# H2 rows copied to PSUM by VectorE, outside picks marked through eight bit masks, and the first mixers' norm spread behind the next projection tile

## The chip, the cores and the metric

The kernel runs on one core of one Trainium2 chip. The metric is the time of one execution on the device in microseconds (us). A core has five engines that run side by side, each through its own list of instructions in order: TensorE (PE) multiplies matrices into PSUM, VectorE (DVE) and ScalarE (ACT) work elementwise, GpSimd (POOL) works elementwise in SBUF and issues the indirect DMAs (gathers by an index), and SyncE (SP) issues most other DMAs. They wait for each other by semaphores. An instruction that waits holds up everything behind it on its own engine.

## The reference

One layer of a decoder trunk for 512 prompt tokens and 64 sample tokens (width 2048), all in float32. What the change touches:

```python
proj = h @ w_in                               # x_lru | y_gate | sc_b | sc_c | sc_x, 1024 columns each
out_lru = rec * gelu(y_gate)                  # head group A
out_sc = sc_b * causal_conv(sc_c * sc_x)      # head group B
mix = concat([rmsnorm(out_lru, g_lru), rmsnorm(out_sc, g_sc)]) @ w_out
x = x + gate1 * mix
h2 = modulate(rmsnorm(x), shift2, scale2)
# PEER, 8 heads: 2 x 128 keys give 16384 experts of one neuron each, the best 16 a token and head
v1, i1 = top_k(scores[..., 0], 16);  v2, i2 = top_k(scores[..., 1], 16)
expert = i1 * 128 + i2                        # of the best 16 sums v1 + v2, weighted by g = softmax
out = sum(gelu(h2 . expert_u[expert]) * g * expert_v[expert])
x = x + gate2 * out                           # then a last RMSNorm
```

## The kernel before

All activations are kept with channels on the 128 partitions and tokens along the free axis. A float32 matmul is made of three passes over halves of the numbers: hi x hi, hi x lo and lo x hi, with hi made by an ACT copy and lo by a POOL subtraction (for projection weights whi and wlo, for expert weights xhi at L905 and xlo at L906).

**Projections and mixers (to about 945 us).** `project` makes one tile of 128 output channels: 96 pairs of matmuls (two halves of the tokens), 13 us of PE. For head group B each of eight steps makes the tiles c, s and b of one channel tile. Between tiles `ada_turn(n)` puts in up to n pieces of the conditioning matmuls, taken from a list of 64, of which the last seven are kept back in this part. In this stage the order on PE is written by hand; a scheduler places the other engines' instructions.

The RMSNorm of head group A is taken at the first of these steps: `norm_stats` sums the squares on PE and starts a short chain of DVE and ACT instructions on a 128x5 tile (rc_g); the function `spread` that it returns spreads the 576 reciprocal roots over all partitions by small matmuls (st_g, L237 and L239) and two ACT copies (R_g). Then DVE scales the eight tiles of o by it. The norm of group B is taken in the same way after the last step, inside the output projection.

**PEER, the U stage (1204 to 2249 us).** The 80 most used values of i1 (`perm[:L]`, L = 80) are computed densely: for each one block of 128 experts is multiplied with all 512 prompt tokens, in two halves of 24 matmuls into pu, after the second of which ACT writes act (L1377). Picks whose i1 lies outside those 80 are computed row by row: an indirect DMA from POOL (L1204) fetches for each of 128 partitions one expert's row (128x2048, one row slot of five), and DVE multiplies it with the token's H2 row and sums (the dot, L1232, one instruction a row). Rows are ordered in six tiles, of 64 rows for the samples and 34, 47, 37, 30 and 11 for the prompt. For each of the last five tiles the H2 rows of its tokens are fetched once by an indirect DMA (h2r, from a row slot) and copied to a PSUM tile hT by ACT (`use_h`, L1219). hT has one buffer, so that the copy waits for the last dot of the tile before it.

All order in this stage is written by hand in a loop over the 160 halves. It carries a reckoning of DVE time (`spare`): each half adds 5.5 or 6.9 us, rows and pieces of other work subtract what their generator yields as cost. That other work is, in turn:

- `choice`: the last top-k work, then `count`, then a sort of the tokens by how many outside picks they have;
- from its end on (half R1 of the plan), `all_slots`: the lists of rows of each tile; and the pairs of the gate matrix: one-hot tiles op and wr on DVE (L1560), scaled on ACT (L1568), multiplied on PE (gbank, L1574) and copied out by ACT (stg, L1581). They are spread evenly over the halves from R1 to half 140;
- rows, 1 a half before R1 (a little more where DVE is idle), 2 a half after it, and from the end of `all_slots` on (half R2 of the plan) evenly to the end of the stage.

`count` marks the outside picks: fl is 1 where i1 equals one of the 48 keys in `perm[:, L:]`. It reads i1 from PSUM and adds up 48 comparisons of 128x512 numbers:

```python
V.tensor_scalar(fl, i1, perm[:, L:L + 1], None, op0=ALU.is_equal)
for x in range(L + 1, 128):
    V.scalar_tensor_tensor(fl, i1, perm[:, x:x + 1], fl, op0=ALU.is_equal, op1=ALU.add)
```

**PEER, the V stage (to 3202 us).** The same blocks and the rest of the rows with the second weights, then the last norm.

Of the kernel before, what the change touches and what calls it, by code (L numbers as in the profile page):

```python
# [5 lines left out]
F32 = mybir.dt.float32  # L6
F32R = mybir.dt.float32r
I32 = mybir.dt.int32
U32 = mybir.dt.uint32
AF = mybir.ActivationFunctionType  # L10
ALU = mybir.AluOpType
# [17 lines left out]
NA = NP  # L29
NG = T - NA  # L30
NE = 128
L = 80
# [49 lines left out]
def build(ctx, tc, A, O, dbg=None):  # L82
    nc = tc.nc
    V, S, PE, G = nc.vector, nc.scalar, nc.tensor, nc.gpsimd
# [177 lines left out]

    def modulate(src, R, jscale, jshift, k0, nk, nm):

# [28 lines left out]
    x = big.tile([128, KD, T], F32, name="x", tag="big")  # L293
    for q in range(4):
        nc.sync.dma_start(x[:, 4 * q:4 * q + 4, :], A["xt"][:, 4 * q:4 * q + 4, :])
    st = []
# [55 lines left out]
    def ada_turn(n, keep=7):  # L352

        for a in pend:
            ada_out(*a)
        pend.clear()
        for _ in range(min(n, len(todo) - keep)):
            a = todo.pop(0)
            ada_mm(*a)
            if a[2] == 3:  # L360
                pend.append(a[:2])
                break
# [6 lines left out]
    for hc in range(4):  # L369
        for j in range(2):  # L370
            for kq in range(4):
                ada_mm(j, hc, kq)
                if hc == j == 0 and kq == 2:
                    spread = norm_stats(st, D, "n1")
                if hc == 0 and j == 1 and kq == 1:
                    R = spread()
# [53 lines left out]
    def project(src, nm):  # L430
        his, los = stream_w(src, nm)
        p = pp.tile([128, 2, 512], F32, name=f"pp_{nm}", tag="pp")
        mm3([p[:, 0, :HT], p[:, 1, :HT]], his, los, movs)
        return p
# [109 lines left out]
    def sc_b(i, p):  # L544
        cv = sc_t[i]
        j = KW + i
        V.tensor_mul(o[:, j, :HT], p[:, 0, :HT], cv[:, :HT])
        V.tensor_mul(o[:, j, HT:NP], p[:, 1, :NX], cv[:, HT:NP])
        V.tensor_mul(s3(o[:, j, NP:]), s3(p[:, 1, NX:HT]), smp(cv, CO, 2, 0, 8))
# [22 lines left out]
    st = []  # L572
    for i in range(KW):
        square_sum(o[:, i, :], i, st, "g0")
    for i in range(KW):
        sc_c(i, project(A["w_in"][24 + i], f"c{i}") if i else pc0)
        ada_turn(2)
        sc_x(i, project(A["w_in"][32 + i], f"s{i}"))
        if i == 0:
            spread = norm_stats(st, W, "g0")  # L580
        ada_turn(2)
        if i == 0:
            R = spread()
            st = []
            for k in range(KW):
                V.scalar_tensor_tensor(o[:, k, :], o[:, k, :], cols[:, C_GN + k:C_GN + k + 1], R, op0=ALU.mult, op1=ALU.mult)
        sc_b(i, project(A["w_in"][16 + i], f"b{i}"))
        ada_turn(2)
        square_sum(o[:, KW + i, :], i, st, "g1")
    for k in range(KW):  # L590
# [2 lines left out]
    def out_half(k, hf):  # L593
        hi, lo = half_w(A["w_out"][k], f"o{k}", hf)
        mm3([p_out[k][:, i, :HT] for i in range(2)], (hi, hi), (lo, lo), movs, range(8 * hf, 8 * hf + 8))
# [2 lines left out]
    out_half(0, 0)  # L598
    spread = norm_stats(st, W, "g1")
    out_half(1, 0)  # L600
    ada_turn(2)
    R = spread()
    for k in range(KW, KD):
        V.scalar_tensor_tensor(o[:, k, :], o[:, k, :], cols[:, C_GN + k:C_GN + k + 1], R, op0=ALU.mult, op1=ALU.mult)
        split(hv[0][:, k, :], hv[1][:, k, :], o[:, k, :], G if k % 3 == 1 else V)
# [7 lines left out]
    st = []  # L613
# [20 lines left out]
    spread = norm_stats(st, D, "n2")  # L634
    ada_turn(1, 0)
    R = spread()
# [6 lines left out]
    def pbank(tag, nm, bufs):  # L643
        return psum["p"].tile([128, 512], F32, name=nm, tag=tag, bufs=bufs)
# [39 lines left out]
    rt = p2.enter_context(tc.tile_pool(name="rt", bufs=1))  # L684
# [4 lines left out]
    perm = rt.tile([128, 128], F32, name="perm")  # L689
# [32 lines left out]
    rq = p2q.enter_context(tc.tile_pool(name="rq", bufs=1))  # L722
# [116 lines left out]
    for i in range(RB):  # L839
        r, k = new_row(f"row0_{i}")  # L840
# [146 lines left out]
    h = HD - 1  # L987
# [67 lines left out]
    def count():  # L1055

        m = nd["m"] = rt.tile([128, 3, QT], F32, name="nd_m")
        fc = rq.tile([128, 2, NA], F32, name="flags", tag="oh", bufs=2)
        fl, code = fc[:, 0, :], fc[:, 1, :]
        i1, i2 = pbank("g", "i1", 2), iselP[:, 1, :]  # L1060
        S.activation(i1, iselP[:, 0, :], AF.Copy)
        yield None
        V.tensor_scalar(fl, i1, perm[:, L:L + 1], None, op0=ALU.is_equal)
        for x in range(L + 1, 128):
            V.scalar_tensor_tensor(fl, i1, perm[:, x:x + 1], fl, op0=ALU.is_equal, op1=ALU.add)
            if x % 8 == 7:
                yield 5.0
        V.scalar_tensor_tensor(code, i1, 128.0, i2, op0=ALU.mult, op1=ALU.add)
        V.scalar_tensor_tensor(code, code, 1.0, fl, op0=ALU.add, op1=ALU.mult)
        V.tensor_reduce(m[:, 0, :], fl.rearrange("p (z k) -> p z k", k=NPK), axis=AX.X, op=ALU.add)  # L1070
        for z in range(QT):
            V.tensor_scalar(m[:, 1, z:z + 1], rowi, float(128 * z), None, op0=ALU.add)
        V.scalar_tensor_tensor(m[:, 2, :], m[:, 0, :], float(NA), m[:, 1, :], op0=ALU.mult, op1=ALU.add)
        yield 5.0
        yield None
        for z in range(QT):
            G.dma_start(pickd[z * 128:(z + 1) * 128, 0:NPK], code[:, z * NPK:(z + 1) * NPK])
            G.dma_start(pickd[z * 128:(z + 1) * 128, NPK:], topv[z].rearrange("p h k -> p (h k)"))
        for _ in range(2):
            yield None  # L1080
# [126 lines left out]
    def gather_u(i):  # L1207
        p0, n, c = GT[i]
        held, st = {}, {}

        def fetch_h():
            held["h"] = new_row(f"h2r{i}")
            G.indirect_dma_start(out=held["h"][0], out_offset=None, in_=h2d,
                                 in_offset=bass.IndirectOffsetOnAxis(ap=tok[:, i:i + 1], axis=0))

        def use_h():
            st["h"] = psum["h"].tile([128, D], F32, name=f"hT{i}", tag="hT", bufs=1)
            r, a = held.pop("h")
            S.activation(st["h"], r, AF.Copy)  # L1219
            row_log[a] = True  # L1220

        def fetch(j):
            held[j] = new_row(f"u{i}_{j}")
            take(held[j][0], A["u"], rows_i[i][:, j:j + 1])

        def dot(j):
            if j == 0:
                st.setdefault("h", first_h["h"])
                dots[i] = actp.tile([128, c], F32, name=f"dots{i}", bufs=1)
            r, a = held.pop(j)  # L1230
            row_log[a] = True
            V.scalar_tensor_tensor(r, r, 1.0, st["h"], op0=ALU.mult, op1=ALU.mult, accum_out=dots[i][:, j:j + 1])  # L1232

        if i:
            fetches.append(fetch_h)
            uses.append(use_h)
        for j in range(c):
            fetches.append(lambda j=j: fetch(j))
            uses.append(lambda j=j: dot(j))
# [372 lines left out]
    for n in range(NU2):  # L1612
        _, i, c = stream[n]
# [110 lines left out]
    for m in range(M):  # L1724
# [8 lines left out]
        for kq in range(KD // VQ):  # L1733
# [7 lines left out]
            if (m, kq) in tplan:  # L1741
                t = len(fin["tok"])
                r = new_row(f"tok{t}")[0]
# [24 lines left out]
    R, Rp = drive(token_norm(fin["sq"], NA, "a", vp, norm_banks("a")))  # L1768
# [13 lines left out]
    with tc.If(any_ > 0), tc.tile_pool(name="fb", bufs=1) as fp:  # L1782
        io1 = fp.tile([128, 128], F32, name="f_io1")
        V.tensor_scalar(io1, iota, 1.0, None, op0=ALU.add)
        for i, (p0, n, c) in enumerate(GT):
# [4 lines left out]
            h = fp.tile([128, D], F32, name=f"f_h{i}", tag="h", bufs=1)  # L1790
# [4 lines left out]
            w = kk[:, 1, :]  # L1795
# [11 lines left out]
            for t_ in ("u", "v"):  # L1807
                for j in range(NPK):
                    r = gp.tile([128, D], F32, name=f"f_{t_}{i}_{j}", tag=f"row{j % RB}", bufs=1)
# [11 lines left out]
        for t in range(QT):  # L1821
            r = gp.tile([128, D], F32, name=f"f_tok{t}", tag=f"row{t}", bufs=1)
# [16 lines left out]
        R = drive(token_norm(sqs, NA, "f", fp, norm_banks("f")))  # L1839
# [71 lines left out]
```

## Time and profile before

| what | us |
|---|---|
| median of 3 runs | 3227.81 (3214.77 to 3230.24) |
| the profiled execution | 3228.61 |
| its span, first to last instruction | 3226.7 |
| PE busy | 3078.9 (95%) |
| DVE, ACT, POOL busy | 2161.6 (67%), 1052.2 (33%), 1697.2 (53%) |
| PE busy in 1200 to 1460 | 260.0 of 260 |
| PE busy in 1520 to 1700 | 174.0 of 180 |
| PE busy in 1700 to 1900 | 183.9 of 200 |
| PE busy in 1900 to 2100 | 196.7 of 200 |

Times are counted from the first instruction. A line of a profile reads: source line, engine, operation, what is written and what is read, sizes, count; behind it busy time and the mean duration in ns, then the idle time of the engine just before and what ended it. In a timeline the first two numbers are start and duration, and the bracket holds the idle time before and its releaser. Matmul pieces are modelled and overlap, so a busy PE only says that work was queued there.

### The profile page before, as it was taken

Reading aid. Unit: us, or ns where it says so; the run is one execution under the profiler, and the core shown is the slowest. Engines: PE = TensorE matmul, PEld = TensorE weight load, DVE = VectorE, ACT = ScalarE, POOL = GpSimd, SP = SyncE. Lnnn points to the kernel's source line nnn. Section 1 sums busy time; section 2 is a strip of 40 time slices with the busy share of each in tenths; the row PEclk is TensorE's granted clock in tenths of the full one; section 3 lists DMA queues with packets and bytes.
Section 4 is the critical chain, followed back from the end, with each engine's and each line's share of the span. In section 5 each row is a group of like instructions: output and inputs, shape, how many; then the busy total and the mean of one; then the engine's idle time right before and its main releaser. Section 6 shows DMA issues by size and latency. Waiting matters only on the chain.

```text
span 3226.7 us, 46647 instructions
## 1 busy us (share of the span) xinstructions
PE 3078.9 (95%) x17239; PEld 2617.8 (81%) x17239; DVE 2161.6 (67%) x3265; ACT 1052.2 (33%) x1645; POOL 1697.2 (53%) x1001
## 2 busy tenths in 40 slices
PE   6999999999989999999999989999999999999997
PEld 2688889899979998887887868887788878778786
DVE  3465521142245897887988988866677888779855
ACT  3334311122232232222565645542322221222222
POOL 2333233344334235667565656656667676767742
PEclk9999999999989999999999989999999999999998
DMA  9743466534332127889889989979999999999964
GB/s 393 270 149 134 164 213 211 203 119 139 127 126 81 68 90 260 311 307 377 328 311 382 377 332 359 400 285 381 371 387 376 398 333 351 341 388 355 374 215 157
DMA packets 297067, 882.84 MB, mean 274 GB/s; under 512 B 37590, under 2 KB 79446, under 8 KB 245366
## 3 DMA queue, kind: packets, MB, share of 16 engines
q1 hardware_dynamic: 160608, 380.39, 33.1%
q0 software_dynamic: 66336, 413.41, 32.5%
q10 hardware_dynamic: 69888, 86.00, 7.5%
q8 instruction: 136, 2.23, 0.3%
q14 instruction: 99, 0.81, 0.1%
HBM read 879.89 MB, written 66.81 MB: 293 GB/s over the span
## 4 chain that ended last, share of the span: by engine, by line
PE 68%; DMA 15%; POOL 5%; DVE 5%; issue 5%; ACT 1%; SPq 1%; ACTq 0%; POOLq 0%; DVEq 0%
PE pu L1374 20%; PE pv L1394 15%; PE pp_o L140 6%; DMA gsb<-gd 5%; DMA raw<-v 5%; PE pp_c L140 3%; PE pp_s L140 3%; PE qa L140 3%; PE pp_b L140 3%; PE qb L140 3%; POOL xlo L906 2%; PE pp_x L140 2%; PE pp_y L140 2%; PE ada L190 2%; PE gbank L1574 2%
## 5 line engine op out<-in xcount | busy, mean ns | idle before, releaser
L906 POOL TENSOR_TENSOR xlo<-raw,xhi 128x1024 fp32r<-128x1024 f32 x320 | 775.1, 2432 | 497.7 <-ACT xhi L905 485.5
L905 ACT ACTIVATE xhi<-raw 128x1024 fp32r<-128x1024 f32 x320 | 337.0, 1060 | 874.1 <-PE pv L1394 300.1
L1232 DVE SCALAR_TENSOR_TENSOR u<-u,hT 128x2048 f32<-128x2048 f32 x223 | 504.9, 2282 | 128.7 <-DMA u<-u,rows 116.3
L1259 DVE SCALAR_TENSOR_TENSOR accB<-v,dots,accB 128x2048 f32<-128x2048 f32 x211 | 496.3, 2352 | 110.7 <-DMA v<-v,rows 108.4
L1394 PE MATMUL pv<-ahi,xhi 128*128 128x512 f32 x1280 | 513.6, 401 | 17.9 <-ACT xhi L905 11.8
L1394 PE MATMUL pv<-ahi,xlo 128*128 128x512 f32 x1280 | 511.3, 399 | 10.8 <-POOL xlo L906 10.8
L1374 PE MATMUL pu<-hhi,xhi 128*128 128x512 f32 x1280 | 516.5, 404 | 1.4 <-ACT xhi L905 1.4
L1394 PE MATMUL pv<-alo,xhi 128*128 128x512 f32 x1280 | 507.7, 397 | 0.0
L1374 PE MATMUL pu<-hlo,xhi 128*128 128x512 f32 x1280 | 505.7, 395 | 0.0
L1374 PE MATMUL pu<-hhi,xlo 128*128 128x512 f32 x1280 | 503.9, 394 | 1.7 <-POOL xlo L906 1.7
L1394 PEld LDWEIGHTS pv<-ahi,xhi 128*128 128x128 f32 x1280 | 244.5, 191 | 76.8 <-ACT xhi L905 15.4
L1204 POOL DMA_INDIRECT u<-u,rows x223 | 224.3, 1006 | 155.1 <-DVE u L1232 96.3
L1394 PEld LDWEIGHTS pv<-ahi,xlo 128*128 128x128 f32 x1280 | 244.4, 191 | 71.5 <-POOL xlo L906 14.8
L1394 PEld LDWEIGHTS pv<-alo,xhi 128*128 128x128 f32 x1280 | 244.7, 191 | 55.4
L1374 PEld LDWEIGHTS pu<-hhi,xlo 128*128 128x128 f32 x1280 | 242.3, 189 | 56.8 <-POOL xlo L906 2.5
L1374 PEld LDWEIGHTS pu<-hhi,xhi 128*128 128x128 f32 x1280 | 242.8, 190 | 52.3 <-ACT xhi L905 1.8
L1204 POOL DMA_INDIRECT v<-v,rows x223 | 251.5, 1128 | 59.5 <-issue 35.0
L1374 PEld LDWEIGHTS pu<-hlo,xhi 128*128 128x128 f32 x1280 | 242.8, 190 | 47.5
L1574 PEld LDWEIGHTS gbank<-wr,op 128*128 128x128 f32 x1024 | 135.6, 194 | 38.1 <-ACT stg L1581 27.5
L1568 ACT ACTIVATE op<-op,it 128x128 f32<-128x128 f32 x512 | 154.5, 388 | 9.7 <-DVE op L1560 9.7
L1574 PE MATMUL gbank<-wr,op 128*128 128x80 f32 x1024 | 132.2, 272 | 25.4 <-ACT stg L1581 25.3
L1416 DVE TENSOR_TENSOR acc<-acc,pv 128x512 f32<-128x512 f32 x144 | 96.7, 681 | 72.4 <-PE pv L1394 72.4
(481 smaller groups left out, 5410.7 us busy)
## 6 DMA issues: line engine op xcount, KB each, us to landing
wa<-w_ada SPq DMA_DIRECT2D x96, 1024.0 KB, 8.0
raw<-ut SPq DMA_DIRECT2D x160, 512.0 KB, 7.8
raw<-v SPq DMA_DIRECT2D x320, 256.0 KB, 8.5
actd<-act ACTq DMA_DIRECT2D x80, 256.0 KB, 7.4
gd<-stg ACTq DMA_DIRECT2D x64, 320.0 KB, 12.1
gsb<-gd ACTq DMA_DIRECT2D x80, 256.0 KB, 15.9
actr<-actd ACTq DMA_DIRECT2D x40, 512.0 KB, 10.9
raw_o<-w_out SPq DMA_DIRECT2D x32, 512.0 KB, 3.4
```

Source lines behind the costliest of these rows:

```text
L140: PE.matmul(o, st, mv[pick](k), start=first, stop=last)
L190: PE.matmul(acc[32 * g:32 * g + 32, :], cpad[:, 4 * kq + g, :], w[:, g, :], start=kq == 0, stop=kq == 3)
L905: S.activation(hi, raw, AF.Copy)
L906: G.tensor_sub(lo, raw, r32(hi))
L1204: G.indirect_dma_start(out=out, out_offset=None, in_=src, in_offset=bass.IndirectOffsetOnAxis(ap=idx, axis=0), bounds_check=NE * 128 - 1, ...
L1232: V.scalar_tensor_tensor(r, r, 1.0, st["h"], op0=ALU.mult, op1=ALU.mult, accum_out=dots[i][:, j:j + 1])
L1259: V.scalar_tensor_tensor(st["a"], r, dots[i][:, j:j + 1], st["a"], op0=ALU.mult, op1=ALU.add)
L1374: PE.matmul(pu, st[:, kk, :], movA[mv](k), start=k == 0 and a == 0, stop=k == KD - 1 and a == 2)
L1394: PE.matmul(pv, st, mv, start=first and j == 0 and a == 0, stop=last and not end and j == SG - 1 and a == 2)
L1416: V.tensor_add(ak, ak, pv)
L1568: S.activation(ops[:, j0 + j, :], ops[:, j0 + j, :], AF.Copy, scale=it[2][:, b * 4 + j:b * 4 + j + 1])
L1574: PE.matmul(pg[:, j * L:(j + 1) * L], ops[:, j0 + j, :], wr[:, j0 + j, :], start=True, stop=True)
```

## The change

- The copy of a tile's H2 rows to PSUM (`use_h`) is made by DVE instead of ACT.
- `count` marks outside picks through bit masks. A key k is split into its word k >> 4 and its bit k & 15. For each of the eight words a mask `mk[:, w]` is summed from the 48 outside keys (8 instructions on 48 numbers, after six that prepare them). Then for the 512 picks of a partition the mask of the pick's word is chosen (one comparison times mask for each word, added up), shifted right by the pick's bit, and its last bit is the mark. The costs yielded to the reckoning are 4.0, 2.5, 4.5, 6.0 and 5.0 in place of six times 5.0 and 5.0.
- For group A, the tile b of the first step is projected ahead of `spread`, and o is scaled after `sc_b`. For group B, `spread` comes ahead of `ada_turn(2)`, and a second `ada_turn(2)` follows.

```diff
         ada_turn(2)
+        pb_ = project(A["w_in"][16 + i], f"b{i}")
         if i == 0:
             R = spread()
             st = []
+        sc_b(i, pb_)
+        if i == 0:
             for k in range(KW):
                 V.scalar_tensor_tensor(o[:, k, :], o[:, k, :], cols[:, C_GN + k:C_GN + k + 1], R, op0=ALU.mult, op1=ALU.mult)
-        sc_b(i, project(A["w_in"][16 + i], f"b{i}"))
...
     out_half(1, 0)
+    R = spread()
     ada_turn(2)
-    R = spread()
+    ada_turn(2)
...
+        wb = rq.tile([128, 2, NA], U32, name="words", tag="oh", bufs=2)
+        word, bit = wb[:, 0, :], wb[:, 1, :]
...
+        V.memset(ki[:, 0, :], 1)
+        V.tensor_copy(ki[:, 1, :], perm[:, L:])
+        V.tensor_scalar(ki[:, 2, :], ki[:, 1, :], 15, None, op0=ALU.bitwise_and)
+        V.tensor_tensor(ki[:, 0, :], ki[:, 0, :], ki[:, 2, :], op=ALU.logical_shift_left)
+        V.tensor_scalar(ki[:, 1, :], ki[:, 1, :], 4, None, op0=ALU.logical_shift_right)
+        V.tensor_copy(kf, ki[:, 0:2, :])
+        for w in range(8):
+            V.scalar_tensor_tensor(kt, kf[:, 1, :], float(w), kf[:, 0, :], op0=ALU.is_equal, op1=ALU.mult,
+                                   accum_out=mk[:, w:w + 1])
+        yield 4.0
         yield None
-        V.tensor_scalar(fl, i1, perm[:, L:L + 1], None, op0=ALU.is_equal)
-        for x in range(L + 1, 128):
-            V.scalar_tensor_tensor(fl, i1, perm[:, x:x + 1], fl, op0=ALU.is_equal, op1=ALU.add)
-            if x % 8 == 7:
-                yield 5.0
+        V.tensor_copy(bit, i1)
+        V.tensor_scalar(word, bit, 4, None, op0=ALU.logical_shift_right)
+        V.tensor_copy(code, word)
+        V.tensor_scalar(bit, bit, 15, None, op0=ALU.bitwise_and)
+        V.tensor_scalar(fl, code, 0.0, mk[:, 0:1], op0=ALU.is_equal, op1=ALU.mult)
+        yield 2.5
+        for w in range(1, 8):
+            V.tensor_scalar(word.bitcast(F32), code, float(w), mk[:, w:w + 1], op0=ALU.is_equal, op1=ALU.mult)
+            V.tensor_add(fl, fl, word.bitcast(F32))
+            if w == 4:
+                yield 4.5
+        V.tensor_copy(word, fl)
+        V.tensor_tensor(word, word, bit, op=ALU.logical_shift_right)
+        V.tensor_scalar(word, word, 1, None, op0=ALU.bitwise_and)
+        V.tensor_copy(fl, word)
+        yield 6.0
...
         def use_h():
-            S.activation(st["h"], r, AF.Copy)
+            V.tensor_copy(st["h"], r)
```

What the order of the instructions shows of it, at three places. First PE between the tiles s0 and b0 of head group B, before the change (pc_g: sums of squares; ada: a conditioning piece):

```order
L140 MATMUL pp_s0_3095<-hhi_78,wlo_s0_1_3093 128x288 x2
L229 MATMUL pc_g0_3204<-ones_68,sqa_g0_3037 128x1 x5
L190 MATMUL ada4_0_3070<-wa4_0_3_3224,cpad_105 32x512 x4
L237 MATMUL st_g0_0_3233<-ident_76,rc_g0_3210 128x128 x4
L239 MATMUL st_g0_1_3234<-ident_76,rc_g0_3210 128x64
L140 MATMUL pp_b0_3262<-hhi_78,whi_b0_0_3252 128x288 x2
```

and after it, at the end of tile b0:

```order
L140 MATMUL pp_b0_3244<-hhi_78,wlo_b0_1_3242 128x288 x2
L237 MATMUL st_g0_0_3342<-ident_76,rc_g0_3210 128x128 x4
L239 MATMUL st_g0_1_3343<-ident_76,rc_g0_3210 128x64
L200 MATMUL pm4_0_3362<-ident_76,part4_0_3230 128x128 x4
L190 MATMUL ada4_1_3372<-wa4_1_0_3373,cpad_105 32x512 x4
```

The two spreading matmuls have moved behind all of b0. At the second norm (st_g1, between the tiles o1 and o0 of the output projection) PE's order is the same in both kernels.

Second, ACT at the start of the second prompt tile of rows, before (hT2 is the PSUM tile, xhi85 the high part of the 85th half, stg3 the gate matrix on its way out):

```order
L1377 ACTIVATE act40_15689<-pu40_15609 128x512
L1378 DMA actd_8627<-act40_15689 128x512
L905 ACTIVATE xhi84_15697<-raw84_15639 128x1024
L1581 ACTIVATE stg3_15472<-gbank_14168 128x4x80
L1568 ACTIVATE op34_15595<-op34_15595,it2_13591 128x128 x8
L1219 ACTIVATE hT2_15752<-h2r2_15551 128x2048
L1581 ACTIVATE stg3_15472<-gbank_14168 128x4x80
L905 ACTIVATE xhi85_15800<-raw85_15692 128x1024
```

and DVE at the same tile, after:

```order
L1176 SCALAR_TENSOR_TENSOR kk3_15618<-R3_14442,kk3_15618 128x128
L1250 COPY hT2_15640<-h2r2_15441 128x2048
L1263 SCALAR_TENSOR_TENSOR u2_0_15628,dots2_15646<-u2_0_15628,hT2_15640 128x2048
L1263 SCALAR_TENSOR_TENSOR u2_1_15632,dots2_15646<-u2_1_15632,hT2_15640 128x2048
L1591 TENSOR_TENSOR op38_15702<-kb_14004,it1_13429 128x1024
```

The copy has left the queue in which stg and xhi stand and is now just ahead of the tile's first dot.

Third, ACT at the start of the pairs (kb holds the keys for the one-hot tiles), before:

```order
L1377 ACTIVATE act28_14153<-pu28_14085 128x512
L1378 DMA actd_8627<-act28_14153 128x512
L905 ACTIVATE xhi60_14161<-raw60_14110 128x1024
L1547 ACTIVATE kb_14165<-perm_8615 128x80
L1548 ACTIVATE kb_14165<-iota_72 128x128
L905 ACTIVATE xhi61_14246<-raw61_14156 128x1024
```

and after:

```order
L1408 ACTIVATE act26_13992<-pu26_13924 128x512
L1409 DMA actd_8627<-act26_13992 128x512
L908 ACTIVATE xhi56_14000<-raw56_13949 128x1024
L1578 ACTIVATE kb_14004<-perm_8615 128x80
L1579 ACTIVATE kb_14004<-iota_72 128x128
L908 ACTIVATE xhi57_14085<-raw57_13995 128x1024
```

The pairs begin behind block 26 instead of block 28, that is four halves sooner (R1 is half 53 instead of 57); the slot lists end at half 131 instead of 136, and the rows stand some six rows further along in the halves between.

More of the change, by code (lines that the diff above doesn't have):

```diff
@@ L1059, in count @@
         fl, code = fc[:, 0, :], fc[:, 1, :]
+        wb = rq.tile([128, 2, NA], U32, name="words", tag="oh", bufs=2)
+        word, bit = wb[:, 0, :], wb[:, 1, :]
         i1, i2 = pbank("g", "i1", 2), iselP[:, 1, :]
         S.activation(i1, iselP[:, 0, :], AF.Copy)
-        yield None
-        V.tensor_scalar(fl, i1, perm[:, L:L + 1], None, op0=ALU.is_equal)
-        for x in range(L + 1, 128):
-            V.scalar_tensor_tensor(fl, i1, perm[:, x:x + 1], fl, op0=ALU.is_equal, op1=ALU.add)
-            if x % 8 == 7:
-                yield 5.0
+        NX_ = 128 - L
+        ki = rq.tile([128, 3, NX_], U32, name="ki", tag="v", bufs=2)
+        kf = rq.tile([128, 2, NX_], F32, name="kf", tag="cand", bufs=2)
+        mk = rt.tile([128, 8], F32, name="mk")
+        V.memset(ki[:, 0, :], 1)
[4 more added lines that the diff above has]
+        V.tensor_copy(kf, ki[:, 0:2, :])
+        kt = rq.tile([128, NX_], F32, name="kt", tag="v", bufs=2)
+        for w in range(8):
+            V.scalar_tensor_tensor(kt, kf[:, 1, :], float(w), kf[:, 0, :], op0=ALU.is_equal, op1=ALU.mult,
+                                   accum_out=mk[:, w:w + 1])
+        yield 4.0
+        yield None
+        V.tensor_copy(bit, i1)
[14 more added lines that the diff above has]
+        yield 6.0
         V.scalar_tensor_tensor(code, i1, 128.0, i2, op0=ALU.mult, op1=ALU.add)
```

## The prediction

> **What bounds the kernel now.** I read the page first, then the waits of TensorE (PE), the chain of waits, the timeline at PE's stops, and busy time by windows. The page:
>
> ```profile
> span 3226.7 us, 46647 instructions
> PE 3078.9 (95%) x17239; PEld 2617.8 (81%) x17239; DVE 2161.6 (67%) x3265; ACT 1052.2 (33%) x1645; POOL 1697.2 (53%) x1001
> ```
>
> PE is the bound: 147.8 us of the span are not PE. Only its stops can be won, so I look at what ends them. From the waits of PE (columns: total us, times, longest):
>
> ```profile
> PE ada L190 <- DMA wa<-w_ada: 30.3, 10, 18.4
> PE gbank L1574 <- ACT stg L1581: 25.3, 4, 14.1
> ...
> PE st_g L237 <- DVE rc_g L150: 3.7, 1, 3.7
> ```
>
> The first is the start of the kernel and is not touched. The other two are. The 25.3 us are three stops in the U stage, and the timeline shows what ScalarE (ACT) did ahead of each:
>
> ```profile
> 1699.43 1.88 ACT L1219 ACTIVATE hT<-h2r 128x2048 f32<-128x2048 f32 x1 [4.73 <-DMA h2r<-h2d,tok]
> 1702.00 2.00 PE L1574 MATMUL gbank<-wr,op 128*128 128x80 f32 x8 [7.77 <-ACT stg L1581]
> 1875.55 1.88 ACT L1219 ACTIVATE hT<-h2r 128x2048 f32<-128x2048 f32 x1 [17.73 <-DVE u L1232]
> 1880.13 2.00 PE L1574 MATMUL gbank<-wr,op 128*128 128x80 f32 x8 [14.08 <-ACT stg L1581]
> 2012.28 1.88 ACT L1219 ACTIVATE hT<-h2r 128x2048 f32<-128x2048 f32 x1 [2.92 <-DVE u L1232]
> 2014.85 1.12 PE L1574 MATMUL gbank<-wr,op 128*128 128x80 f32 x8 [3.25 <-ACT stg L1581]
> ```
>
> ACT stands at the copy of a tile's H2 rows until the rows have landed or VectorE (DVE) has done the last dot of the tile before (one PSUM buffer). Behind it in ACT's queue wait the stg copy that PE needs and the next xhi. The five copies fall on gather tiles 1 to 5; two of them stop nobody.
>
> What a stop costs in all is read from act, which ACT writes at the end of each second half:
>
> ```profile
> 1590.90 0.60 ACT L1377 ACTIVATE act<-pu 128x512 f32<-128x512 f32 x1 [2.00 <-PE pu L1374]
> 1687.01 0.60 ACT L1377 ACTIVATE act<-pu 128x512 f32<-128x512 f32 x1
> 1725.20 0.60 ACT L1377 ACTIVATE act<-pu 128x512 f32<-128x512 f32 x1 [1.99 <-PE pu L1374]
> 1848.70 0.60 ACT L1377 ACTIVATE act<-pu 128x512 f32<-128x512 f32 x1 [1.25 <-PE pu L1374]
> 1893.73 0.60 ACT L1377 ACTIVATE act<-pu 128x512 f32<-128x512 f32 x1 [2.68 <-PE pu L1374]
> 2004.38 0.60 ACT L1377 ACTIVATE act<-pu 128x512 f32<-128x512 f32 x1 [4.74 <-PE pu L1374]
> 2036.84 0.60 ACT L1377 ACTIVATE act<-pu 128x512 f32<-128x512 f32 x1 [4.71 <-PE pu L1374]
> ```
>
> From 1590.90 to 1687.01 lie 14 halves: 6.86 us each, PE's own pace. From 1687.01 to 1725.20, 1848.70 to 1893.73 and 2004.38 to 2036.84 lie four halves each, 27.4 us of work; they take 38.2, 45.0 and 32.5. So the stops cost 10.8 + 17.6 + 5.1 = 33.5 us, 8.4 more than the gaps, because PE starts again slowly:
>
> ```profile
> 1700.00:1720.00 20.00, 18.00 (x87) 15.43 (x87) 15.05 (x29) 11.10 (x21) 13.02 (x11) 0.85 0.85 328
> 1740.00:1760.00 20.00, 20.00 (x105) 17.02 (x104) 18.07 (x17) 12.22 (x26) 12.82 (x10) 1.00 1.01 421
> ```
>
> (PE, weight loads, DVE, ACT, POOL busy; granted clock; DMA share; GB/s.) The clock is 0.85 behind the first stop. The second row shows the other thing to see: DVE at 90% and the DMA engines full.
>
> **The H2 copies.** Would PE win the 33.5 us? Not if the row work on DVE is late as well. The order places two rows (dots) in each half there. Windows of the dot's line (x counts two instructions a row):
>
> ```profile
> 1590.00:1690.00 100.00, 62.85 (x55) 1.00 0.84 335
> 1720.00:1850.00 130.00, 81.82 (x72) 1.00 0.97 400
> 1895.00:2009.00 114.00, 72.92 (x64) 1.00 0.94 373
> 2020.00:2098.00 78.00, 45.57 (x40) 1.00 1.00 401
> ```
>
> That is 27.5, 36, 32 and 20 rows, or 7.27, 7.22, 7.12 and 7.80 us for two; over all 115.5 rows in 422 us, 7.31. PE needs 6.86. So between stops the rows fall behind PE by 0.26 to 0.45 us a half. What happens when they are far behind is seen on GpSimd (POOL), which issues the rows and makes xlo in one queue:
>
> ```profile
> 1675.80 1.00 POOL L1204 DMA_INDIRECT u<-u,rows  x1 [3.06 <-DVE u L1232]
> ...
> 1684.67 7.10 POOL L906 TENSOR_TENSOR xlo<-raw,xhi 128x1024 fp32r<-128x1024 f32 x3
> 2095.28 2.41 POOL L906 TENSOR_TENSOR xlo<-raw,xhi 128x1024 fp32r<-128x1024 f32 x1 [3.66 <-ACT xhi L905]
> ```
>
> At 1675.80 POOL waits 3.06 us for DVE to free a row slot. The xlo of the next half queues behind the row and the first of the three ends at about 1687.1, just when PE finishes the half before it (act at 1687.01): no reserve is left. At 2095.28 POOL waits for ACT instead and the rows hold nobody. So the stops gave the rows time which they had in part needed. With the copy on DVE, ACT no longer waits, but POOL's queue does, from about half 80 on.
>
> The copy on DVE: the trace has none. Bounds: ACT's 1.88 us and the SBUF-to-PSUM pass of L1256 below, 2.35 us; I take 2.35, the same engine and the same two memories. Ahead of a tile's first dot DVE had to wait for the copy anyway, but did other work meanwhile, so I count it in full. Nobody but the next dot and the pairs (op, wr) stands behind it on DVE.
>
> Sum for the U stage from half 82 to half 131, where the order stops placing two rows a half: stops removed -33.5; rows holding PE back 50 halves x (7.20 - 6.86) = +17, with 7.20 between the two stretches that had no reserve (7.27, 7.22) and the best (7.12), since a PE that is held back also asks the full DMA queues for less; three copies inside, 3 x 2.35 = +7. Net -9.5, ends -13.5 (7.12) and -4 (7.31).
>
> **The marks.** Prices from the groups of DVE (busy, mean ns):
>
> ```profile
> L1065 DVE SCALAR_TENSOR_TENSOR flags<-i,perm,flags 128x512 f32<-128x512 f32 x47 | 35.3, 751 | 1.5
> L1101 DVE TENSOR_SCALAR ohs<-io,rk 128x512 f32<-128x512 f32 x4 | 1.9, 486 | 0.1
> L1428 DVE COPY sqs<-sqs 128x512 f32<-128x512 f32 x1 | 0.4, 426 | 0.7 <-ACT sqs L1422 0.7
> L1416 DVE TENSOR_TENSOR acc<-acc,pv 128x512 f32<-128x512 f32 x144 | 96.7, 681 | 72.4 <-PE pv L1394 72.4
> L778 DVE SCALAR_TENSOR_TENSOR f<-f x8: 210/224/226, 1100.4 to 1341.7; 128x64 f32<-128x64 f32 x8
> L772 DVE CAST f<-sh 128x192 f32<-128x192 uint32 x4 | 5.4, 1347 | 0.1
> L1256 DVE TENSOR_SCALAR accB<-v,dots 128x2048 f32<-128x2048 f32 x6 | 14.1, 2354 | 0.4
> ```
>
> Removed: 48 x 0.75 = 36 us. Added at full length: the PSUM cast 0.75; eleven scalar passes x 0.49 = 5.4; three casts x 0.43 = 1.3; eight two-tensor passes x 0.68 = 5.4; and the 14 small ones on 48 keys x 0.3 = 4.2: 17 us. But the removed passes read one SBUF tensor and PSUM and all took the same time, while the cast L772, SBUF to SBUF, took 0.26 us at best and 1.35 in the mean: it meets POOL's xlo of 2.4 us. The marks come in four pieces, each likely to meet one xlo: 17 + 4 x 2.4 = 27. At worst the xlo of each of the eight halves they lie in meets them: 17 + 8 x 2.4 = 36, nothing saved (the third rival). By the first two figures 9 to 19 us of DVE are saved, at a place (1388 to 1440) where PE never stops: worth nothing there. The planner counts 22 us instead of 35 and starts the pairs four halves sooner (22 us of PE at 5.5 before the pairs), with three rows fewer done (3 x 2.35 = 7). DVE therefore comes to the pairs between 4 us earlier and 6 us later relative to PE. I take 0. Its cover is the waiting for rows which DVE does before that stage.
>
> The Trainium skill ("SBUF — State Buffer", Who interferes with whom) says that VectorE and GpSimd share one port pair as an exclusive lock, taken for the whole instruction by copies, casts and scalar passes within SBUF, and held against two-input SBUF passes. L772 and L1065 agree. By that rule, which speaks against this part, the worst case above would be nearer than my middle one, and the sum would be 9 us less of a gain.
>
> **The first mixers' norm.** Now, on PE:
>
> ```profile
> 371.24 1.90 PE L237 MATMUL st_g<-ident,rc_g 128*128 128x128 f32 x8 [3.70 <-DVE rc_g L150]
> 372.94 0.53 PE L239 MATMUL st_g<-ident,rc_g 128*128 128x64 f32 x2
> 373.46 13.51 PE pp_b L140 x96
> 389.26 12.97 PE pp_c L140 x96
> ```
>
> With the spread behind tile b0, the 3.70 us gap is filled; b0 no longer starts slowly (13.51 - 12.97 = 0.54), and the spread itself need not (1.90 + 0.53 against an estimated 2.0): -4.6, between -3.7 and -5.2. What is late next: DVE scales o some 10 us later, and the next square sum shares R's buffer and waits for that on ACT; the whi passes behind it have a tile's time (13 us). I count 0.
>
> The second norm's part changes nothing: ada_turn keeps seven pieces back, seven are left and none is pending there, so both turns issue nothing, and the order reads the same.
>
> **Sum.** -9.5 - 4.6 + 0 = -14 against the profiled execution's own 3228.6 us (span 3226.7): 3215 rounded up. The median of the runs, 3227.8, lies 0.8 below that execution; one run is at 3214.8, so about 0.5% (16 us) is what a measurement of this kernel tells from no change.
>
> **Rivals.** (1) The rows keep up, and all stops go. For it: the rows' pace of 7.12 in one stretch, and DMA idle in others. Against it: POOL's queue at 1684.67 had no reserve before any stop. It would give 3228.6 - 33.5 - 4.6 = 3190. (2) The rows take back all the U stage gains: pace 7.31 and two more copies or late marks of 5 us: 33.5 - 22.5 - 7 - 5, about nothing. 3224 to 3230. (3) Slower: the marks, locked out by xlo, save nothing, while the pairs come four halves sooner; DVE then comes to them 22 - 7 = 15 us late, and at pace 7.31 the U stage loses 22.5 + 7 + 15 - 33.5 = 11: 3235. It decides once the marks take more than about 31 us.
>
> **Chances.** Mine (3204 to 3224) 0.52; rival 1, 0.16; rival 2, 0.18; rival 3, 0.10; something else 0.04. Of mine about four tenths lies below 3212, so faster by over 0.5% is 0.16 + 0.21 + 0.02 = 0.39; slower by over 0.5% needs more than rival 3's middle: 0.06; the rest 0.55. The range from rival 1's middle to past rival 2: 3192 to 3232.
>
> **What would show it.** Right: no row in which PE gbank waits for ACT stg behind a copy; a DVE copy of 2.2 to 2.4 us five times; PE waiting in small pieces for xlo (POOL) or xhi between half 80 and 131; the st_g row without a gap. Wrong: PE busy without waits through 1650 to 2100 (rival 1), or marks of over 31 us and PE waits longer than 33 us there (rival 3).

## The result and the profile after

| | us |
|---|---|
| before, median of 20 runs | 3223.49 (3214.77 to 3235.44) |
| after, median of 20 runs | 3204.41 (3192.43 to 3217.03) |
| ratio, 95% interval | 0.9945, 0.9931 to 0.9958 |
| profiled execution after | 3200.89 (before 3228.61) |

The change makes the kernel 0.55% faster, about 18 us; 3215, within 3192 to 3232, was forecast. The two profiled executions lie 27.7 us apart, 10 more than the ratio gives: that of before is 5 above its median, that of after 4 below. So sizes are read below from stages, and totals from the ratios.

First the page of after, then the longest waits of PE over the whole run (total us, times, longest; pv is the PSUM tile of the V stage's matmuls):

```profile
span 3199.1 us, 46649 instructions
PE 3067.4 (96%) x17239; PEld 2606.4 (81%) x17239; DVE 2167.9 (68%) x3267; ACT 1044.3 (33%) x1640; POOL 1701.2 (53%) x1001
...
PE ada L190 <- DMA wa<-w_ada: 30.6, 12, 18.4
PE pv L1425 <- ACT xhi L908: 15.7, 4, 7.6
PE pv L1425 <- POOL xlo L909: 11.4, 9, 2.8
PE pv L1425 <- DVE acc L1447: 8.2, 4, 5.2
PE gbank L1605 <- ACT stg L1612: 7.4, 10, 3.2
```

The 25.3 us of gbank behind stg have become 7.4, in ten pieces of at most 3.2, and the st_g row is gone from the list. The five copies, by the line's own view (ns min/median/max), and the norm's spread on PE, from the timeline:

```profile
L1250 DVE COPY hT<-h2r x5: 2284/2286/2295, 1555.7 to 2092.5; 128x2048 f32<-128x2048 f32 x5
...
380.46 1.05 PE L237 MATMUL st_g<-ident,rc_g 128*128 128x128 f32 x8
381.35 0.33 PE L239 MATMUL st_g<-ident,rc_g 128*128 128x64 f32 x2
```

The copy costs 2.29 us, and st_g stands behind tile b0 with no idle time ahead of it. It is also faster itself: 1.05 us where the same eight matmuls took 1.90. The windows say why (busy us of PE, weight loads, DVE, ACT, POOL; granted clock; DMA share; GB/s): first before, right behind the gap, then after.

```profile
371.00:374.00 3.00, 2.76 (x13) 2.79 (x14) 0.17 (x2) 0.71 (x2) 0.00 (x0) 0.57 1.02 391
...
380.00:383.00 3.00, 3.00 (x31) 2.23 (x33) 1.72 (x5) 1.77 (x3) 1.43 (x1) 1.00 0.04 16
```

Behind the 3.70 us stop the clock was 0.57, now it is 1.00. The Trainium skill ("TensorE: Matmul & The Clock Gate", Part 1) says that PE falls to half its clock after an idle window of about 3.4 us; the 3.70 us stop agrees with it.

What is left in the U stage. The ends of second halves, read from act (halves 71, 97 and 137), first in before, then in after:

```profile
1618.43 0.60 ACT L1377 ACTIVATE act<-pu 128x512 f32<-128x512 f32 x1 [2.08 <-PE pu L1374]
1807.53 0.60 ACT L1377 ACTIVATE act<-pu 128x512 f32<-128x512 f32 x1 [2.03 <-PE pu L1374]
2106.82 0.60 ACT L1377 ACTIVATE act<-pu 128x512 f32<-128x512 f32 x1 [2.08 <-PE pu L1374]
...
1618.90 0.60 ACT L1408 ACTIVATE act<-pu 128x512 f32<-128x512 f32 x1 [1.20 <-PE pu L1405]
1808.25 0.60 ACT L1408 ACTIVATE act<-pu 128x512 f32<-128x512 f32 x1 [2.64 <-PE pu L1405]
2082.24 0.60 ACT L1408 ACTIVATE act<-pu 128x512 f32<-128x512 f32 x1 [4.86 <-PE pu L1405]
```

In after, a half takes 7.28 us from 1618.90 to 1808.25 (26 halves), and from there to 2082.24 it takes 6.85 (40 halves), PE's own pace, although two of the five copies lie in this second stretch (at 1850.9 and 1981.5). So PE is held in the first stretch only, and it costs 26 x (7.28 - 6.86) = 11 us. Before took 189.1 and 299.3 us for the same two stretches, after 189.3 and 274.0: all that the U stage wins lies in the second. (Ahead of half 71 after takes 4.9 us longer, because the pairs begin sooner: 163 of their matmuls stand there against 123.) The first of the three stops at copies, in the first stretch, was replaced by other waits of the same total. Which, is shown by the longest stop of PE, by what ACT waited for (total, times, longest) in 1570 to 1820, and by ACT at that stop.

```profile
1799.98 0.67 PE L1605 MATMUL gbank<-wr,op 128*128 128x80 f32 x4 [3.23 <-ACT stg L1612]
...
ACT op L1599 <- DVE op L1591: 28.7, 18, 4.6
...
1796.88 1.57 ACT L1599 ACTIVATE op<-op,it 128x128 f32<-128x128 f32 x5 [4.62 <-DVE op L1591]
```

PE waits for stg on ACT; ACT stands at the scaling of a pair's one-hot tile; and DVE makes that tile late. Two dots stand just ahead of it on DVE, and ahead of these the end of a tile's row list (5.4 us from 1785.86). It is the old wait with another instruction in the copy's place.

The marks on DVE, grouped:

```profile
L1090 DVE TENSOR_SCALAR words<-flags,mk 128x512 f32<-128x512 f32 x7 | 6.3, 895 | 0.2
L1091 DVE TENSOR_TENSOR flags<-flags,words 128x512 f32<-128x512 f32 x7 | 4.8, 693 | 0.2
L1085 DVE CAST flags<-words 128x512 f32<-128x512 uint32 x1 | 2.5, 2523 | 0.0
L1096 DVE TENSOR_SCALAR words<-words 128x512 uint32<-128x512 uint32 x1 | 2.5, 2509 | 0.0
L1079 DVE SCALAR_TENSOR_TENSOR kt<-kf 128x48 f32<-128x48 f32 x8 | 1.7, 208 | 0.3
...
L1084 DVE TENSOR_SCALAR words<-words 128x512 uint32<-128x512 uint32 x1 | 0.4, 428 | 0.0
L1097 DVE CAST flags<-words 128x512 f32<-128x512 uint32 x1 | 0.4, 427 | 0.0
```

With the small groups that are not printed here counted in, the marks take 23.1 us where the comparisons took 36.0. The two casts L1085 and L1097 have the same form and took 2.52 and 0.43 us. The timeline shows the long one beside POOL:

```profile
1389.54 2.52 DVE L1085 CAST flags<-words 128x512 f32<-128x512 uint32 x1
...
1389.38 2.39 POOL L909 TENSOR_TENSOR xlo<-raw,xhi 128x1024 fp32r<-128x1024 f32 x1 [0.65 <-ACT xhi L908]
```

It began 0.16 us after xlo and ended 0.3 us after xlo's end.

### The profile page after: what moved, and what is told of

It is laid out like the page before. It is cut to its first block, busy times and chain, and to the rows that moved or that the text cites. A ratio compares the mean times of both kernels' runs of the same rounds, so it can differ in the third digit from the quotient of the medians.

```text
span 3199.1 us, 46649 instructions
## 1 busy us (share of the span) xinstructions
PE 3067.4 (96%) x17239; PEld 2606.4 (81%) x17239; DVE 2167.9 (68%) x3267; ACT 1044.3 (33%) x1640; POOL 1701.2 (53%) x1001
## 4 chain that ended last, share of the span: by engine, by line
PE 73%; DMA 11%; POOL 5%; issue 5%; DVE 4%; ACT 1%; SPq 1%; ACTq 0%; POOLq 0%; DVEq 0%
PE pu L1405 20%; PE pv L1425 18%; PE pp_o L140 6%; DMA raw<-v 4%; DMA gsb<-gd 4%; PE pp_c L140 3%; PE pp_s L140 3%; PE qa L140 3%; PE pp_b L140 3%; PE qb L140 3%; POOL xlo L909 3%; PE ada L190 2%; PE pp_x L140 2%; PE pp_y L140 2%; PE gbank L1605 2%
## 5 line engine op out<-in xcount | busy, mean ns | idle before, releaser
L1235 POOL DMA_INDIRECT v<-v,rows x223 | 253.5, 1137 | 57.9 <-issue 38.7
L129 POOL TENSOR_TENSOR wlo_o<-raw_o,whi_o 128x1024 fp32r<-128x1024 f32 x32 | 77.5, 2423 | 119.9 <-ACT whi_o L127 119.9
```

The source lines that it names most:

```text
L129: lo_engine(share).tensor_sub(lo, raw, r32(hi))
L1235: G.indirect_dma_start(out=out, out_offset=None, in_=src, in_offset=bass.IndirectOffsetOnAxis(ap=idx, axis=0), bounds_check=NE * 128 - 1, ...
```

## The experiments

Where a run's time lies is read from its trace by four stages: to the first matmul into pu, from there to act of half 153 (the U stage without its end), to the first matmul into pv, and to the end. All are single executions; 3 us of the first column come and go before the first tile c, whatever the change (its first matmul stands at 334.3 to 335.7 in six traces, at 337.8 to 338.3 in eight); the ratio (95% interval) is that of timed runs against runs of before on the same chip.

| run | to pu | U stage | to pv | V stage | profiled, us | ratio |
|---|---|---|---|---|---|---|
| before | 1193.7 | 1011.1 | 39.8 | 982.1 | 3228.61 | 1 |
| after | 1189.3 | 991.4 | 34.0 | 984.4 | 3200.89 | 0.9945 (0.9931 to 0.9958) |
| after again | 1189.9 | 996.2 | 34.4 | 992.7 | 3215.05 | 0.9938 (0.9915 to 0.9961) |
| copy alone | 1194.6 | 990.7 | 37.3 | 982.6 | 3207.06 | 0.9960 (0.9945 to 0.9975) |
| norm alone | 1186.9 | 1011.3 | 37.4 | 978.0 | 3215.41 | 0.9979 (0.9962 to 0.9996) |
| marks alone | 1198.1 | 1017.0 | 37.0 | 990.5 | 3244.42 | 1.0037 (1.0021 to 1.0052) |
| marks alone, old costs | 1199.3 | 1010.1 | 38.7 | 974.4 | 3224.34 | 1.0006 (0.9988 to 1.0023) |
| after, old marks | 1189.8 | 994.9 | 36.5 | 984.2 | 3207.18 | 0.9937 (0.9920 to 0.9954) |
| after, old costs | 1192.0 | 988.7 | 37.4 | 986.6 | 3206.48 | 0.9908 (0.9889 to 0.9926) |
| the same again | 1192.3 | 990.2 | 35.8 | 977.0 | 3197.13 | 0.9931 (0.9905 to 0.9958) |
| after, 1.85 rows | 1192.1 | 979.5 | 44.3 | 999.4 | 3217.06 | 0.9935 (0.9916 to 0.9954) |
| old costs, 1.93 rows | 1192.5 | 980.0 | 41.6 | 994.0 | 3210.14 | 0.9936 (0.9914 to 0.9959) |
| old costs, two copies | 1192.0 | 991.5 | 40.5 | 976.8 | 3202.58 | 0.9937 (0.9914 to 0.9960) |
| after, half dots | 1189.5 | 985.1 | 40.8 | 965.2 | 3182.48 | 0.9880 (0.9857 to 0.9904) |

With ACT copies and the plan of before, the U stage took 1010.1 to 1011.3 us in three runs; in the seven with DVE copies, whole dots and 2 rows a half it took 988.7 to 996.2, two of them of the kernel after, 4.8 apart. So differences of some 5 us and more can be read from it. The V stage cannot be read so: two executions of the kernel after lie 8.3 apart there.

**The copy alone.**

```diff
 # before
-            S.activation(st["h"], r, AF.Copy)
+            V.tensor_copy(st["h"], r)
```

> Before, with only the H2 copy moved to VectorE. Theory A, the prediction on record: the rows cannot keep two a half below 7.20 us, so TensorE loses 17 + 7 us of the 33.5 it wins: -9.5 us, ratio 0.997, and waits spread over halves 82 to 131. Theory B, from the trace after: VectorE's own work is under TensorE's pace, the waiting for rows shrinks once VectorE is late, and rows hold TensorE only while VectorE is at its limit of about 17 us behind (halves 71 to 97 there, 11 us): about -20 us, ratio 0.994; from half 97 on TensorE at 6.9 us a half with three copies on VectorE.

The ratio, 0.9960, is between the two theories; the U stage, shorter by 20.4, is theory B's, and beyond the bound of -13.5 that the prediction gave its term. PE's waits from 1560 to 2110, and the longest stop's cause on ACT:

```profile
PE gbank L1574 <- ACT stg L1581: 5.5, 3, 3.6
PE pu L1374 <- POOL xlo L906: 0.5, 1, 0.5
...
1717.63 2.45 ACT L1568 ACTIVATE op<-op,it 128x128 f32<-128x128 f32 x8 [7.00 <-DVE op L1560]
```

The 25.3 us of stops have become 6.0. Waits spread over halves 82 to 131 (theory A) are not there: halves 97 to 137 take 279.0 us, or 6.97 each.

**The first norm alone.**

```diff
 # before
         ada_turn(2)
+        pb_ = project(A["w_in"][16 + i], f"b{i}")
         if i == 0:
             R = spread()
             st = []
+        sc_b(i, pb_)
+        if i == 0:
             for k in range(KW):
...
-        sc_b(i, project(A["w_in"][16 + i], f"b{i}"))
```

> Before, with only the first norm's spread behind tile b0. Prediction on record: -4.6 us (ratio 0.9986), the st_g row without a gap, everything behind it 4 to 5 us earlier up to the U stage. Rival: the ScalarE copies and VectorE scaling that come later cost it back at the next square sum: 0.

0.9979, which excludes 0, though only just. The trace is sharper: from the start of the first step's tile c to the output projection's first matmul lie 357.4 us, against 362.7 in before and with the copy alone, and 357.3 in after. That is -5.4 to within 0.1, and the rival's cost further on does not appear.

**The marks alone.** Before, with `count` from the kernel after, its costs included; then the same with costs of the old sum, which leaves the plan as it was:

```diff
 # both runs, on before
-        V.tensor_scalar(fl, i1, perm[:, L:L + 1], None, op0=ALU.is_equal)
-        for x in range(L + 1, 128):
...
+        V.tensor_copy(bit, i1)
+        V.tensor_scalar(word, bit, 4, None, op0=ALU.logical_shift_right)
...
 # the second run only
-        yield 2.5
+        yield 8.0
...
-                yield 4.5
+                yield 9.0
...
-        yield 6.0
+        yield 9.0
```

> Before, with only the bit masks and their costs in the plan (pairs four halves sooner, ScalarE still copies the H2 rows). Prediction on record: 0, within -4 to +6 us; marks 17 to 27 us of VectorE instead of 36. Rival (locked out by GpSimd): marks over 31 us, later slower by 5 to 10. Third: the freed VectorE time gives the pairs a start with less lag, so the stops at the copies shorten: -3 to -8.

> Before, with the bit masks but their costs in the plan brought up to the old 35 + 5, so that pairs and rows stand at the halves of before; ScalarE still copies the H2 rows. Theory P (the plan): marks alone cost 12 us only because pairs and rows came sooner, to a VectorE that was not ahead: ratio 1.000, within 0.002. Theory M (the marks themselves, locked out by GpSimd, or their memory): still 1.003 to 1.005.

Alone, the marks make the kernel slower, 1.0037; with the old costs 1.0006. The instructions are the same, so what costs would be the plan (theory P): less cost booked, pairs and rows four halves sooner. The U stage agrees, 1017.0 against 1010.1, in one execution each. The two ratios are of different chips and their intervals just touch, and below the ratio of one kernel moves by 0.0023 between two chips, so this is likely rather than shown. PE's gbank waits between 1500 and 2200, marks alone first, then with the old costs, and the four longest stops of marks alone:

```profile
PE gbank L1602 <- ACT stg L1609: 27.8, 8, 12.5
...
PE gbank L1602 <- ACT stg L1609: 22.9, 4, 13.0
...
1691.38 2.00 PE L1602 MATMUL gbank<-wr,op 128*128 128x80 f32 x8 [7.11 <-ACT stg L1609]
1811.74 1.12 PE L1602 MATMUL gbank<-wr,op 128*128 128x80 f32 x8 [2.08 <-ACT stg L1609]
1865.71 1.57 PE L1602 MATMUL gbank<-wr,op 128*128 128x80 f32 x6 [12.46 <-ACT stg L1609]
2003.07 1.35 PE L1602 MATMUL gbank<-wr,op 128*128 128x80 f32 x5 [3.95 <-ACT stg L1609]
```

The three stops at copies stay about as long as they were (23.5 us, 25.1 in before); a new one of 2.08 and small ones come with them.

**After with the old marks and their costs.**

```diff
 # after
-        V.tensor_copy(bit, i1)
-        V.tensor_scalar(word, bit, 4, None, op0=ALU.logical_shift_right)
...
+        V.tensor_scalar(fl, i1, perm[:, L:L + 1], None, op0=ALU.is_equal)
+        for x in range(L + 1, 128):
+            V.scalar_tensor_tensor(fl, i1, perm[:, x:x + 1], fl, op0=ALU.is_equal, op1=ALU.add)
+            if x % 8 == 7:
+                yield 5.0
```

> After, with the 48 comparisons and their costs put back (copy on VectorE and the norm stay). If the marks are worth nothing, as on record: the same as after, ratio to before about 0.9945. If the marks' saved 13 us of VectorE go into a smaller lag at half 65, this one holds TensorE longer: ratio 0.996 to 0.998.

0.9937, as after (0.9945 and 0.9938): with the copy on DVE, the marks are worth nothing that can be measured, as forecast.

**After with the old costs**, twice (the three `yield` lines above), and after itself again.

> After, with the same old costs: the masks, but pairs and rows at the halves of before. If the sooner pairs and rows cost time here too, ratio 0.992 to 0.993, less lag at half 65 than after has and fewer waits between halves 65 and 97. If with the copy on VectorE the plan's shift is indifferent: as after, 0.9945.

> The kernel after once more, beside the next three on one chip: ratio 0.9945 again. In the U stage ScalarE waits for VectorE's one-hot tiles of the pairs (some 29 us between 1570 and 1820) and TensorE loses 10 to 12 us between halves 65 and 137.

> After with the marks' old costs, once more, on the same chip as after. If sooner pairs and rows cost time with the copy on VectorE too: 8 to 12 us faster than after (ratio to before 0.991). If its first ratio was that chip's before: the same as after within 4 us.

The first ratio, 0.9908, looked like a version that beats the change, clear of its interval. On one chip with it, after measured 0.9938 and this version 0.9931: no difference that these runs can tell. The first ratio's own median, 3199.85, is the second's, 3200.05; it was before that measured 3229.14 on one chip and 3224.43 on the other. The U stages, 988.7 and 990.2 against 991.4 and 996.2, hint at 4 us for the sooner pairs and rows, but after with the old marks, whose pairs and rows also stand at the halves of before, took 994.9: not shown. In the second execution of after, ACT waited 25.3 us for one-hot tiles between 1570 and 1820, and halves 71 to 97 took 189.2 us, as in the first (28.7 and 189.3). Where it is longer is seen on PE, on POOL ahead of it, and on DVE at the start and the end of a row list:

```profile
1527.55 0.50 PE L1405 MATMUL pu<-hhi,xlo 128*128 128x512 f32 x1 [3.81 <-POOL xlo L909]
...
1521.89 1.00 POOL L1235 DMA_INDIRECT u<-u,rows  x1 [9.72 <-DVE u L1263]
1524.10 0.99 POOL L1235 DMA_INDIRECT u<-u,rows  x1 [1.21 <-DVE u L1263]
1525.12 2.37 POOL L909 TENSOR_TENSOR xlo<-raw,xhi 128x1024 fp32r<-128x1024 f32 x1
...
1507.15 0.22 DVE L1170 TENSOR_SCALAR sl<-R 128x128 uint32<-128x128 uint32 x1
1519.34 2.28 DVE L1263 SCALAR_TENSOR_TENSOR u<-u,hT 128x2048 f32<-128x2048 f32 x1
```

A row waits 9.72 us for DVE to free its slot, xlo stands behind it, and PE stops for 3.81. This is the prediction's way from POOL's queue to PE, once, at the start of the pairs, where it had not been expected. What makes DVE late is not the dots: from 1507.15 to 1519.34 it makes the row list of a tile (`all_slots`), 12.2 us without a dot. In the first execution of after the same list took 9.5 us, POOL waited 5.48 for a slot, and PE did not stop.

**Fewer rows a half.** After with 1.85, and after with the old costs and 1.93, from the first pairs on. The rest of the rows come later in the stage.

```diff
-RATE = (1.0, 2.0)
+RATE = (1.0, 1.85)
```

> After, with 1.85 rows a half instead of 2 from the first pairs on (the rest come in the later halves, which have fewer). Theory A' (rows hold TensorE at halves 65 to 97 because VectorE is at its limit): TensorE comes to 6.9 us a half there, -8 to -11 us, ratio 0.991 to 0.992. If something else holds TensorE there (the pairs themselves, or full DMA queues): as after, 0.9945. If it takes from V-stage cover (rows done later): slower.

> After with the old costs and 1.93 rows a half instead of 2 up to half 127. If the remaining 13 us between halves 65 and 137 are VectorE at its limit, this wins 4 to 8 of them; 4 rows fewer are done by half 145, which at most half of gives back in the V stage (1.85 gave back all): ratio 0.990 or a little under. If the late rows cost as much as the early ones: as with the old costs alone.

The U stage wins 12 us with 1.85 (979.5 against 991.4) and about 9.5 with 1.93; the ratios, 0.9935 and 0.9936, are no better than those of after (0.9945 and 0.9938); on the chip of 1.85 the old costs at 2 rows measured 0.9908. With 1.93 no wait of PE over 0.1 us is left from 1560 to 2140. PE's waits from 2150 to 2250, the end of the U stage, and ACT there:

```profile
PE pv L1425 <- ACT acc L1445: 8.0, 1, 8.0
PE pu L1405 <- POOL xlo L909: 5.0, 3, 2.3
PE pv L1425 <- POOL xlo L909: 3.6, 2, 2.4
...
2247.08 1.09 ACT L1445 ACTIVATE acc<-pv 128x512 f32<-128x512 f32 x2 [12.65 <-DMA gsb<-gd]
```

PE waits 18 us there (with the old costs at 2 rows, 8 from 2150 to 2270). The rows put off come in the last halves of the stage, where the V stage's first loads come too, and ACT stands 12.65 us until a load of gsb (a block of the gate matrix) has landed. What the rows save early seems to be lost late; the V stage is long in both profiled executions as well, 994.0 and 999.4 against 976.8 to 992.7 in the other versions with whole dots that have the copy on DVE. Both executions lie some 6 us above the median of their runs, so how much is lost where is not settled.

**Half dots.** After, with the dots over the first 1024 channels:

```diff
-            V.scalar_tensor_tensor(r, r, 1.0, st["h"], op0=ALU.mult, op1=ALU.mult, accum_out=dots[i][:, j:j + 1])
+            V.scalar_tensor_tensor(r[:, :D // 2], r[:, :D // 2], 1.0, st["h"][:, :D // 2], op0=ALU.mult, op1=ALU.mult,
+                                   accum_out=dots[i][:, j:j + 1])
```

> After, with dots over the first 1024 channels only (the other half of each dot product is left out): 1.15 us of VectorE a row instead of 2.28, all fetches as they are. If VectorE's work sets the rows' pace: no TensorE waits from half 65 to 140, 6.9 us a half, -11 us, ratio 0.991. If the round trip of a row (slot free, issue, landing through full DMA queues) sets it: TensorE still held between halves 71 and 97, -0 to -4 us.

From 1592 to 1808: after, then half dots, and what DVE waited for in each (total, times, longest).

```profile
1592.00:1808.00 216.00, 208.75 (x1064) 173.50 (x1063) 197.76 (x280) 122.31 (x264) 131.98 (x90) 0.99 0.93 373
...
1592.00:1808.00 216.00, 211.64 (x1096) 177.61 (x1096) 138.67 (x281) 125.46 (x276) 133.54 (x92) 1.00 0.93 372
...
DVE u L1263 <- DMA u<-u,rows: 18.0, 17, 1.7
...
DVE u L1263 <- DMA u<-u,rows: 74.0, 43, 3.4
```

59 us of DVE's work are gone, 56 come back as waiting for rows, and PE is busy for only 2.9 us more in this window; the U stage, 985.1, wins 6 of the 11. So both answers hold in part: with the dots at half their length DVE waits for rows to land instead (at a DMA share of 0.93), and ACT still waits 16.0 us for one-hot tiles, against 28.7. How much of the other 5 us is the round trip of a row (slot free, issue, landing) and how much the row lists, which stay whole, no run separates. The V stage is 19 us shorter than in after; why was not tried.

**Two copies.** After with the old costs, and

```diff
             V.tensor_copy(st["h"], r)
+            V.tensor_copy(st["h"], r)
```

> After with the old costs and every H2 copy made twice, the price of the copy on VectorE by itself. By the prediction's term each copy between halves 82 and 131 costs TensorE its full 2.3 us: +7 us against the old costs alone. If VectorE's reserve takes it up except where it stands at its limit: 0 to +3 us.

The ratio is 0.9937 against 0.9931; the U stage is 1.3 to 2.8 us longer than with one copy, not 7 (and two executions of one kernel can lie 4.8 apart): DVE's reserve takes up most of it.

## Why the prediction was right, and where it was not

- **The total**, 3204, lies in the range, at the lower edge of the likeliest case's own (3204 to 3224), and the ratio's 18 us are near the 14 forecast. That is partly luck of the reference: the sum was made against an execution 5 us above the median, and from there 24 us are gone, not 14. One term of the sum was far off: the net gain of the U stage, -9.5 forecast and at most -13.5, is -15 and -20 in the two executions of after.
- **The stops at the copies** went, and five copies of 2.29 us stand on DVE, as forecast. The 33.5 us for them fit: the two runs with fewer rows, in which PE hardly waits in this stage, take 979.5 and 980.0, 31 us less than before. After wins 20 of these 31, all behind half 97, and 11 remain.
- **Rows holding PE** is the step that was mis-sized: +17 for rows and +7 for three copies. Measured are 11 us for both in after, in halves 71 to 97 instead of 82 to 131. The failed step is the pace of 7.20 us for two rows, carried over 50 halves. It was read from stretches in which DVE also waited for rows. It held up to half 97 (7.28), where DVE waited as before (18.0 us in 1592 to 1808); behind half 97 that waiting shrank, and PE kept its own pace. The waits of DVE in before (1720 to 1850) and in after (1800 to 1930):

```profile
DVE u L1232 <- DMA u<-u,rows: 12.1, 14, 2.1
...
DVE u L1263 <- DMA u<-u,rows: 3.2, 5, 1.2
```

  12.1 us in 19 halves are 0.64 us a half, more than the 0.34 by which the pace was thought to miss. Over all of halves 97 to 137 after waits 13.3 us, 0.33 a half. Why the waiting shrinks there and not sooner is not shown. A pace holds for the state it was read in.
- **How rows hold PE** was only partly right: by POOL's queue and xlo once, in the second execution of after (3.81 us at 1527, behind a row list), and for the rest by ACT, which waits for DVE's one-hot tiles (28.7 us). The same engine that had stood at the copy now stands at the pairs. The prediction names the pairs as standing behind the copy on DVE, but gave ACT's wait for them no cost.
- **The copies' full price** on DVE, 2.3 us each, was wrong: doubled, they cost 1.3 to 2.8 us together.
- **The marks' duration**: 27 forecast, of which 17 uncontended; measured 23.1. L1085, L1096 and two of L1090 lost 7.1 us to xlo, which leaves 16.0. The Trainium skill ("SBUF — State Buffer", Who interferes with whom) says that casts and scalar passes can take a port pair that VectorE shares with GpSimd, as an exclusive lock; the same cast at 0.43 and 2.52 us agrees. By that rule the worst case, an xlo met in each of eight halves, was to be the nearer one; three were met in full and one in part.
- **The marks' value**, 0, holds beside the DVE copy. By themselves they cost 0.37%: rival 3's direction, but not its cause. It was to decide only above 31 us of marks; it came at 23.1, and went with the old costs, in which the marks took longer (25.3). If the plan is the cause, the cover that the prediction counted on, "the waiting for rows which DVE does before that stage", was too small.
- **The first norm**: -5.4 measured, -4.6 forecast within -3.7 to -5.2. The gap gave its 3.70 and b0 0.7; the spread saved 0.9 rather than 0.4, because it had run on the slow clock as well.
- **The second norm** does nothing: from the first matmul of the output projection (pp_o) to the first of the next projection (qa) lie 235.6 us in both traces.
- **Rival 1** (all stops go) did not come: 11 us of PE's time stay lost in halves 71 to 97. **Rival 2** (rows take it all back) did not come either.

Open: the stages give -15 to -20 us for the U stage (996.2 and 991.4 against 1011.1) and -5.4 for the norm, and the six ratios of versions with both and 2 rows a half lie between -18 and -30 us. The V stage's scatter is too wide to say whether anything is given back there, and the plan's part (at most 4 us in the U stage with the DVE copy, 7 with the ACT copy) rests on few executions. How much of the 11 us in halves 71 to 97 comes from the rows and how much from the row lists that DVE makes in the same halves is open as well: fewer rows remove all of it, halved dots half.

## What to carry to other kernels

A pace read beside waits is not an engine's capacity: before it is used for a state in which the engine is late, take the waiting out of it. When an instruction that blocks a queue is taken away, ask which later instruction of the same queue waits for the same late engine, here the pairs' scaling. A better cost in a plan moves work: run the faster code once with the old costs, to tell the code from the plan, and time versions that are to be compared beside each other on one chip.

## What had not been expected of the hardware

Stops much shorter than the 3.4 us of the Trainium skill ("TensorE: Matmul & The Clock Gate", Part 1) can cost the clock too. In before, stops of 1.43 and 1.70 us follow each other within 4 us from 2221.6, and the 6 us behind the second ran at 0.50. A single stop of 1.52 us, at 1957.1 with two copies, left the clock at 1.00, but a single one of 1.92 us in after, up to 3118.4, brought it to 0.72 (windows behind the stops, in this order, columns as above):

```profile
2225.50:2231.50 6.00, 6.00 (x14) 4.74 (x15) 3.35 (x2) 2.04 (x2) 5.05 (x4) 0.50 0.95 244
...
1958.60:1964.60 6.00, 6.00 (x30) 5.11 (x31) 6.00 (x7) 4.57 (x11) 4.40 (x3) 1.00 1.00 413
...
3118.40:3124.40 6.00, 6.00 (x24) 5.03 (x25) 2.87 (x5) 0.63 (x1) 0.00 (x0) 0.72 0.67 167
```

So small stops can be dearer than their gaps. What decides which of them cost the clock is not shown here.
